# Layer 0's attention ends: the splits of the fetched head outputs stand behind the third scores, one between two stages each

## The chip, the core and the metric

One core of a Trainium2 chip runs the whole program once. The metric is device time in microseconds (us); lower is better. TensorE (PE) multiplies, VectorE (DVE) and ScalarE (ACT) read PSUM and SBUF, GpSimd (POOL) works on SBUF, and SyncE (SP) issues most of the DMAs. Each engine works through its own list of instructions; engines meet through semaphores.

## The reference

Two trunk layers over 512 latent and 256 context tokens of width 1024: layer 0 mixes tokens by differential attention, layer 1 by neighbourhood attention, each followed by a squared-ReLU MLP, with adaptive shift, scale and gate. Only the end of layer 0's attention matters here:

```python
def diff_attend(q, k, v, lam):
    s = jnp.einsum('bqhmd,bkhmd->bhmqk', q, k).astype(jnp.float32) * ATTN_SCALE
    p = jax.nn.softmax(s, axis=-1)
    w = (p[:, :, 0] - lam * p[:, :, 1]).astype(v.dtype)
    return jnp.einsum('bhqk,bkhe->bqhe', w, v)

def finish(o):
    B, T = o.shape[:2]
    o = rms_norm(o, subln_g) * (1.0 - lam_init)
    return o.reshape(B, T, D_MODEL) @ w_o
```

The output of all eight heads is multiplied by `w_o`, gated, and added to the residual stream.

## The kernel before

Tokens stand in six tiles of 128: tiles 0 and 1 are context (they read 256 keys), tiles 2 to 5 are latent (768 keys). fp32 matmuls are done in three passes over operands split into a rounded high part and the remainder. So a "split" is two operations: ACT copies the high part, then POOL or DVE subtracts it to get the low part.

**Stages.** `head0` works on one head in stages, named by a letter and a tile:

- `Q0a`, `Q0b`: two halves of the projection of tile 0.
- `U0`, `U2`, `U4`: queries and keys of two tiles are transposed on PE (L499) and split; the keys by L444, L445, L446, L448 in turn, once for each of the two maps, ACT and DVE alternating.
- `S`: scores (L517) into the PSUM tile `PS`, of which there is one; then twice a reduce to the maximum on DVE (L522) and an exp on ACT (L523), and on DVE L526, L528 and L529, which combines the two maps.
- `T`: the weights are transposed (L541) in two halves into two `PB` tiles and split (ACT L543, DVE L544).
- `V`: weights times values (L552) into a `PB` tile, read by ACT L555 and DVE L556; then a norm: ACT L559, DVE L290, a power on POOL (L296), DVE L561.
- `O`: the output is transposed (L569, `PB`), scaled by ACT L570, and every second tile goes to DRAM (L575) or, for the last head, is split in place (ACT L782, DVE L783).

There are two `PB` buffers, handed out in turn to T, V and O in the order of the code.

**The output projection.** `project` fetches the outputs of heads 0 to 6 back from DRAM: `x0` to `x6` (L738, on SP, into tiles `N`, of which there are four). `X0` to `X6` split them: ACT L743, then L744, which POOL does for X0, X1, X3, X4 and X6 and DVE for X2 and X5. `P0a` to `P5b` multiply tile by tile (L750): an `a` part takes heads 0 to 2, a `b` part heads 3 to 5, both into the same `PA` tile, of which there are two; behind a `b` part DVE multiplies by the gate (L755) and adds the residual (L756). The matmuls of heads 6 and 7 come later. `B0` splits the fourth tile of output weights (ACT L145, POOL L146) and fetches the two gates (L723, also `N`). `m` and `n` are the halves of a chunk of the modulation matmul (L257, L263; `PA`).

**Order.** The stages stand in strings written by hand. `run` walks a string and emits each word's instructions; apostrophes mean an earlier head, so in `END0`, where no new head begins, `'` is head 7 and `''` head 6. On PE, POOL and SP the instructions keep the order of the string (`PINNED`), and so do the splits `X`; the other instructions of ACT and DVE are placed by a scheduler when the program is built. `END0` is the string behind head 7's projection, and in the profiled execution it runs from about 424 to 502 us.

Of the kernel before, what the change touches and what calls it, by code (L numbers as in the profile page):

```python
# [40 lines left out]
T0'' Q4b' S2'' V0'' n0 T1'' V1'' S3'' T2'' U0' Q5a' Q5b' m2 O0'' S4'' T3'' n2 w0 w1 Q0a U2' O1'' V2''  # L41
S5'' T4'' Q0b c0 w2 V3'' S0' Q1a O2'' V4'' U4' Q1b c1 w3 O3'' T5'' m3 O4'' S1' T0' V5'' c2 V0' n3 S2' T1'
Q2a O5'' Q2b S3' V1' c3 O0' U0 Q3a T2' Q3b Q4a S4' T3' Q4b V2' Q5a T4' S5' O1' V3' Q5b S0 T5' m1 U2"""
END0 = """x0 x1 x2 x3 S1' O2'' O3'' V4'' T0' U4' n1' X0 V5'' T1' X1 S2' O4'' X2 x4 V0' S3' x5 P0a O5'' T2' X3 P1a
X4 V1' O0' S4' X5 B0 P0b m0 V2' O1' x6 P1b T3' n0 P2a T4' S5' P2b O2' P3a V3' V4' P3b m1 T5' P4a O3' n1
X6 P4b V5' P5a P5b O4' O5'"""
CYCLE1 = """w0 w1 Q0a T3'' U4' Q1a c0 w2 V2'' V3'' Q0b S0' Q1b Q2a S1' Q2b Q3a T0' S2' Q4a c1 w3 T1' Q3b S3' V0' U0
Q4b c2 U2 Q5a T2' Q5b c3 V1'"""
LAST1 = """Q0a T3'' U4' Q1a c0 x0 x1 V2'' V3'' Q0b S0' Q1b X0 x2 Q2a S1' Q2b X1 Q3a T0' S2' Q4a T1' Q3b X2 S3' V0'
# [868 lines left out]
def run(order, c, steps, load, split, **others):  # L918


    for word in order.split():
        kind, num, h = word[0], word[1:].rstrip("'"), c - word.count("'")
        if kind == "w":
            load(h + 1, int(num))
        elif kind == "c":
            split(h + 1, int(num))
        elif kind in others:
            others[kind](num)
        elif h in steps:
            steps[h](kind, 2 * int(num[0]) + (num[1:] == "b") if kind == "Q" else int(num))  # L930


def hybrid_block(tc, a, out):
    nc = tc.nc
    with ExitStack() as ctx, ExitStack() as st:
# [19 lines left out]
        with b.psum_phase("psA", **PS_ATTN0):  # L955
# [12 lines left out]
            with tc.manual_schedule(engines=PINNED):  # L968
                heads[1] = b.head0(1, w[1], hT)
                for c in range(2, HEADS0):  # L970
                    if c == HEADS0 - 1:
# [9 lines left out]
                       "X": lambda n: proj["split"](int(n), (nc.gpsimd, nc.vector)[int(n) % 3 == 2])}  # L981
                run(END0, HEADS0, heads, load, split, **mod, **own)
            proj["end"]()
# [146 lines left out]
```

## Time and profile before

| | |
|---|---|
| median of 3 runs | 1902.31 us (1901.79 to 1906.84) |
| profiled execution | 1902.15 us, of which the span is 1899.6 us |
| mean granted TensorE clock | 0.981 |
| busy over the span | PE 94%, DVE 60%, ACT 44%, POOL 43% |
| busy in 424 to 502 us, PE | L750 31.6 us, L552 12.4 us, L517 10.9 us |
| PE idle there ahead of L517 | 9.2 us, until ACT L523 (5.1) or L446 (4.1) |
| PE idle there ahead of L750 | 5.7 us, until ACT L743 (5.1) or DVE L744 (0.5) |

PE is the busiest engine over the whole span, so its idle times and the clock granted to it are what to read in a short stretch. A busy share says little there: which wait ended last, and what stood in the queue of the engine that was waited for, is in the rows in order of time.

### The profile page before, as it was taken

Reading aid. Unit: us, or ns where it says so; the run is one execution under the profiler, and the core shown is the slowest. Engines: PE = TensorE matmul, PEld = TensorE weight load, DVE = VectorE, ACT = ScalarE, POOL = GpSimd, SP = SyncE. Lnnn points to the kernel's source line nnn. Section 1 sums busy time; section 2 is a strip of 40 time slices with the busy share of each in tenths; the row PEclk is TensorE's granted clock in tenths of the full one; section 3 lists DMA queues with packets and bytes.
Section 4 is the critical chain, followed back from the end, with each engine's and each line's share of the span. In section 5 each row is a group of like instructions: output and inputs, shape, how many; then the busy total and the mean of one; then the engine's idle time right before and its main releaser. Section 6 shows DMA issues by size and latency. Waiting matters only on the chain.

```text
span 1899.6 us, 27132 instructions
## 1 busy us (share of the span) xinstructions
PE 1786.5 (94%) x10256; PEld 1563.8 (82%) x10256; DVE 1133.4 (60%) x2158; ACT 833.7 (44%) x1854; POOL 812.6 (43%) x688
## 2 busy tenths in 40 slices
PE   6989999996999999999999998999998989999998
PEld 5878888884789888888888977989897778888886
DVE  4588777885574343343334676777777664444446
ACT  4476767774342212221221245777676342323321
POOL 3755566653224333342432432433345444444443
PEclk9999999997999999999999998999999999999999
DMA  8122222224324443443432132122212323223232
GB/s 329 42 84 78 87 87 87 79 71 169 119 73 136 132 160 111 167 162 116 148 134 85 56 100 64 57 71 74 65 67 89 117 92 97 89 91 109 90 101 76
DMA packets 66499, 197.61 MB, mean 104 GB/s; under 512 B 8192, under 2 KB 23488, under 8 KB 60224
## 3 DMA queue, kind: packets, MB, share of 16 engines
q1 hardware_dynamic: 58608, 186.03, 29.4%
q10 hardware_dynamic: 7760, 9.85, 1.5%
q8 instruction: 80, 1.31, 0.3%
q14 instruction: 51, 0.42, 0.1%
HBM read 180.74 MB, written 15.11 MB: 103 GB/s over the span
## 4 chain that ended last, share of the span: by engine, by line
PE 75%; DVE 11%; ACT 6%; issue 4%; POOL 2%; DMA 2%; ACTq 0%; SPq 0%; POOLq 0%; DVEq 0%
PE PD L830 22%; PE PA L408 14%; PE PA L865 11%; PE PB L865 9%; PE PA L750 4%; PE PA L257 2%; PE PS L517 2%; PE PB L552 2%; PE PQ L398 1%; PE PS L656 1%; PE PB L701 1%; PE PB L541 1%; PE PB L686 1%; DVE Y L423 1%; ACT W L145 1%
## 5 line engine op out<-in xcount | busy, mean ns | idle before, releaser
L146 POOL TENSOR_TENSOR W<-R,W 128x1024 fp32r<-128x1024 f32 x142 | 351.3, 2485 | 540.6 <-ACT W L145 537.0
L830 PE MATMUL PD<-Q,W 128*128 128x384 f32 (+2 forms) x1992 | 396.0, 346 | 2.4 <-DVE Q L334 1.1
L830 PEld LDWEIGHTS PD<-Q,W 128*128 128x128 f32 x1992 | 345.7, 188 | 33.7 <-issue 8.6
L145 ACT ACTIVATE W<-R 128x1024 fp32r<-128x1024 f32 (+1 forms) x172 | 172.7, 1021 | 450.7 <-PE PA L865 193.6
L865 PE MATMUL PA<-W,H 128*128 128x512 f32 x1080 | 275.4, 393 | 4.6 <-POOL W L146 3.0
L865 PEld LDWEIGHTS PA<-W,H 128*128 128x128 f32 x1080 | 200.1, 188 | 51.3 <-issue 4.5
L839 DVE TENSOR_TENSOR N<-N 128x768 f32<-128x768 f32 (+1 forms) x64 | 66.9, 1046 | 279.2 <-ACT N L835 170.4
L865 PE MATMUL PB<-W,H 128*128 128x512 f32 x840 | 209.2, 391 | 0.0
L865 PEld LDWEIGHTS PB<-W,H 128*128 128x128 f32 x840 | 157.4, 188 | 33.4
L408 PE MATMUL PA<-W,Q 128*128 128x384 f32 (+1 forms) x1008 | 174.3, 325 | 0.4 <-DVE H L621 0.4
L408 PEld LDWEIGHTS PA<-W,Q 128*128 128x128 f32 x1008 | 158.6, 191 | 0.7 <-DVE H L621 0.7
L296 POOL TENSOR_TENSOR SQ<-SQ,half 128x4 f32<-128x4 f32 (+1 forms) x96 | 94.7, 988 | 128.9 <-DVE SQ L421 127.7
L842 DVE SCALAR_TENSOR_TENSOR H<-N,H 128x768 fp32r<-128x768 f32 (+1 forms) x64 | 97.9, 1532 | 25.7 <-ACT H L841 25.0
L408 PE MATMUL PA<-WB,H 128*128 128x384 f32 x576 | 110.9, 345 | 0.8 <-DVE Q L469 0.8
L750 PE MATMUL PA<-W,H 128*128 128x512 f32 x384 | 97.5, 404 | 7.9 <-ACT H L743 5.1
L408 PEld LDWEIGHTS PA<-WB,H 128*128 128x128 f32 x576 | 101.1, 192 | 1.8 <-DVE Q L469 1.1
L830 PE MATMUL PD<-H,W 128*128 128x512 f32 (+1 forms) x408 | 94.1, 378 | 2.4 <-DVE SA L290 2.0
L876 DVE TENSOR_TENSOR H<-PA,H 128x512 f32<-128x512 f32 x78 | 53.8, 690 | 69.7 <-PE PA L865 69.7
L750 PEld LDWEIGHTS PA<-W,H 128*128 128x128 f32 x384 | 71.9, 192 | 25.9 <-ACT H L743 5.4
L523 ACT ACTIVATE E<-PS,SA 128x768 f32<-128x768 f32 (+1 forms) x96 | 72.9, 760 | 36.5 <-DVE SA L522 33.6
L830 PEld LDWEIGHTS PD<-H,W 128*128 128x128 f32 x408 | 73.8, 188 | 18.0 <-DVE H L334 2.9
L517 PE MATMUL PS<-Q,Q 128*128 128x256 f32 (+1 forms) x320 | 70.2, 352 | 19.1 <-ACT Q L446 9.9
(210 smaller groups left out, 3052.6 us busy)
## 6 DMA issues: line engine op xcount, KB each, us to landing
R<-in_w_dram SPq DMA_DIRECT2D x128, 512.0 KB
M<-in_wmod_dram SPq DMA_DIRECT2D x48, 1024.0 KB
R<-in_wqa_dram SPq DMA_DIRECT2D x32, 384.0 KB
R<-in_wqb_dram SPq DMA_DIRECT2D x32, 384.0 KB
Y<-in_rpb_dram SPq DMA_DIRECT2D x48, 128.0 KB
bias<-Y SPq DMA_DIRECT2D x48, 128.0 KB
X<-bias SPq DMA_DIRECT2D x8, 768.0 KB
R<-in_woa_dram SPq DMA_DIRECT2D x8, 512.0 KB
```

Source lines behind the costliest of these rows:

```text
L145: high = nc.scalar.activation(w[:, 0, :n], raw, AF.Copy)
L146: low = (eng or nc.gpsimd).tensor_sub(w[:, 1, :n], raw, w[:, 0, :n].bitcast(F32))
L296: nc.gpsimd.tensor_tensor(r, ss, self.half[:, :n], op=ALU.pow)
L408: nc.tensor.matmul(acc[:, :n], hT[kt][:, x, P * i:P * i + P], w[kt // 2][:, y, o:o + n], start=(kt == 0 and p == 0), stop=(kt == KT - 1 an ...
L517: nc.tensor.matmul(s[:, c0:c1], q[:, m, P * i:P * i + P], k[:, m, c0:c1], start=p == 0, stop=p == 1)
L523: nc.scalar.activation(e[:, m, :nk], s, AF.Exp, bias=mx[:, 0:1], accum_out=sm[:, m:m + 1])
L750: nc.tensor.matmul(ps, oHL[h][:, x, c:c + P], w[h // 2][:, y, 512 * (h % 2):512 * (h % 2) + 512], start=(first and h == hs[0] and p == 0), ...
L830: nc.tensor.matmul(ps[:, at:at + b1 - b0], w[kt // 4][:, x, o:o + P], hT[kt][:, y, b0:b1], start=(kt == 0 and p == 0), stop=(kt == KT - 1 ...
L839: nc.vector.tensor_mul(r, r, r)
L842: nc.vector.scalar_tensor_tensor(u[:, 1, :], r, 1.0, u[:, 0, :].bitcast(F32), op0=ALU.mult, op1=ALU.subtract)
L865: nc.tensor.matmul(ps, hd[:, x, P * i - c0:P * i - c0 + P], w[f][:, y, 512 * n:512 * n + 512], start=(f == 0 and p == 0), stop=(f == len(h ...
L876: nc.vector.tensor_add(av, ps, av)
```

## The change

Only the string `END0` changes. The same words stand in it, 62 of them before and after, so no instruction is added or removed.

```diff
-END0 = """x0 x1 x2 x3 S1' O2'' O3'' V4'' T0' U4' n1' X0 V5'' T1' X1 S2' O4'' X2 x4 V0' S3' x5 P0a O5'' T2' X3 P1a
-X4 V1' O0' S4' X5 B0 P0b m0 V2' O1' x6 P1b T3' n0 P2a T4' S5' P2b O2' P3a V3' V4' P3b m1 T5' P4a O3' n1
-X6 P4b V5' P5a P5b O4' O5'"""
+END0 = """x0 x1 x2 x3 S1' O2'' O3'' V4'' T0' U4' n1' V5'' T1' S2' X0 O4'' V0' X1 S3' O5'' T2' X2 x4 V1' x5 P0a
+O0' S4' X3 P1a X4 B0 V2' T3' O1' X5 x6 P0b m0 S5' T4' P1b n0 P2a O2' V3' P2b T5' P3a V4' P3b m1 O3' P4a n1
+X6 V5' P4b P5a P5b O4' O5'"""
```

X0 and X1 move from before S2' to behind it; X2 moves behind S3', X3 behind S4' as its own neighbour; V1' moves ahead of P0a; V2', T3' and O1' ahead of P0b; S5' and T4' ahead of P1b; V5' ahead of P4b.

ACT, from the first split to the last exp of S2', before (`H` is a split output, `Q` the keys, `E` the exps, `W` the weight of `B0`):

```order
L743 ACTIVATE H_5607<-N_5522 128x768
L555 ACTIVATE O_5623<-PB_5610,SA_5368 128x128
L543 ACTIVATE X_5633<-PB_5634 128x256
L743 ACTIVATE H_5639<-N_5524 128x768
L444 ACTIVATE Q_5163<-PC_5585 64x256
L559 ACTIVATE O_5627,SO_5626<-O_5623 128x128
L446 ACTIVATE Q_5163<-PC_5585 64x256
L444 ACTIVATE Q_5163<-PC_5585 64x256
L446 ACTIVATE Q_5163<-PC_5585 64x256
L570 ACTIVATE OT_5664<-PB_5665,subg 128x128
L743 ACTIVATE H_5668<-N_5526 128x768
L523 ACTIVATE E_5642,SA_5643<-PS_5644,SA_5653 128x768
```

The same place now:

```order
L555 ACTIVATE O_5620<-PB_5607,SA_5368 128x128
L543 ACTIVATE X_5630<-PB_5631 128x256
L444 ACTIVATE Q_5163<-PC_5585 64x256
L559 ACTIVATE O_5624,SO_5623<-O_5620 128x128
L446 ACTIVATE Q_5163<-PC_5585 64x256
L444 ACTIVATE Q_5163<-PC_5585 64x256
L446 ACTIVATE Q_5163<-PC_5585 64x256
L570 ACTIVATE OT_5661<-PB_5662,subg 128x128
L523 ACTIVATE E_5636,SA_5637<-PS_5638,SA_5647 128x768
L555 ACTIVATE O_5670<-PB_5665,SA_5497 128x128
L523 ACTIVATE E_5636,SA_5637<-PS_5638,SA_5650 128x768
L743 ACTIVATE H_5658<-N_5522 128x768
```

The three L743 of X0, X1 and X2 are gone from among the key copies and the first exp; X0 stands behind the second exp, and the L145 of `B0`, which stood between the two exps, is later too.

PE, behind the eight score matmuls of S3', before: P0a, O5'', T2', P1a, V1'.

```order
L750 MATMUL PA_5712<-W_4935,H_5607 128x512 x3
L750 MATMUL PA_5712<-W_4935,H_5639 128x512 x3
L750 MATMUL PA_5712<-W_4981,H_5668 128x512 x3
L569 MATMUL PB_5722<-ident,O_5627 128x128
L541 MATMUL PB_5727<-ident,E_5642 128x128 x3
L541 MATMUL PB_5733<-ident,E_5642 128x128 x3
L750 MATMUL PA_5742<-W_4935,H_5607 128x512 x3
L750 MATMUL PA_5742<-W_4935,H_5639 128x512 x3
L750 MATMUL PA_5742<-W_4981,H_5668 128x512 x3
L552 MATMUL PB_5755<-Q_4967,X_5633 128x256 x4
```

Now: O5'', T2', V1', P0a.

```order
L569 MATMUL PB_5705<-ident,O_5624 128x128
L541 MATMUL PB_5710<-ident,E_5636 128x128 x3
L541 MATMUL PB_5716<-ident,E_5636 128x128 x3
L552 MATMUL PB_5727<-Q_4967,X_5630 128x256 x4
L750 MATMUL PA_5744<-W_4935,H_5658 128x512 x3
L750 MATMUL PA_5744<-W_4935,H_5680 128x512 x3
L750 MATMUL PA_5744<-W_4981,H_5722 128x512 x3
```

P1a no longer stands between T2' and V1', and P0a follows V1'. With two `PB` buffers in turn, V1' (`PB_5727`) writes where T2''s first half (`PB_5710`) was.

DVE around the softmax of S3', now (L522 reduces, L561 ends the norm of V0', L544 splits T2', L744 is X2); before, L744 and L561 stood ahead of both reduces:

```order
L522 TENSOR_REDUCE SA_5694<-PS_5685 128x1
L561 SCALAR_TENSOR_TENSOR O_5674<-O_5670,SO_5677,one 128x128
L522 TENSOR_REDUCE SA_5697<-PS_5685 128x1
L544 TENSOR_TENSOR X_5709<-PB_5710,X_5709 128x384
L544 TENSOR_TENSOR X_5709<-PB_5716,X_5709 128x384
L744 TENSOR_TENSOR H_5722<-N_5526,H_5722 128x768
```

L561 moved in between the two reduces, and the L544 that V1' needs stands behind both. On POOL the power for that L561 (L296) stands between the L744 of X0 and that of X1.

## The prediction

> **What bounds the kernel now.** Read the page first: the span, and the chain that ended last.
>
> ```profile
> span 1899.6 us, 27132 instructions
> PE 75%; DVE 11%; ACT 6%; issue 4%; POOL 2%; DMA 2%; ACTq 0%; SPq 0%; POOLq 0%; DVEq 0%
> ```
>
> Three quarters of the chain are TensorE (PE), so a change on ACT, DVE or POOL counts only where PE waits for it. END0 runs from about 424 to 502 us. The windows of that stretch come next (columns: stretch, length, busy PE, PEld, DVE, ACT, POOL, granted clock, DMA share, GB/s).
>
> ```profile
> 430.00:440.00 10.00, 5.52 (x28) 3.80 (x27) 7.34 (x18) 5.50 (x16) 4.68 (x4) 0.81 0.53 182
> 440.00:450.00 10.00, 6.70 (x21) 5.34 (x21) 5.96 (x11) 5.35 (x12) 1.32 (x1) 0.51 0.49 178
> 450.00:460.00 10.00, 7.83 (x39) 5.71 (x37) 6.36 (x10) 5.55 (x13) 6.13 (x4) 1.00 0.29 98
> 460.00:470.00 10.00, 5.39 (x26) 2.90 (x27) 5.24 (x8) 2.11 (x4) 0.51 (x1) 0.50 0.28 67
> 470.00:480.00 10.00, 10.00 (x54) 7.94 (x54) 5.62 (x12) 3.08 (x9) 0.55 (x1) 0.98 0.63 236
> ```
>
> PE is full only from 470 on. Before that it idles, and in two stretches its granted clock is half. Third, PE's own rows in order of time (start, length, instruction, idle time before it and its releaser): V5'', the last two pieces of S2', V0', S3', P0a, S4', the last two pieces of P0b, m0, O1', P1b, T3'.
>
> ```profile
> 431.30 1.70 PE L552 MATMUL PB<-Q,X 128*128 128x256 f32 x12 [0.35 <-DVE O L556]
> 436.19 1.46 PE L517 MATMUL PS<-Q,Q 128*128 128x256 f32 x4 [2.51 <-ACT Q L446]
> 439.27 1.26 PE L517 MATMUL PS<-Q,Q 128*128 128x512 f32 x2 [1.62 <-ACT Q L446]
> 440.39 1.20 PE L552 MATMUL PB<-Q,X 128*128 128x256 f32 x4
> 444.90 2.93 PE L517 MATMUL PS<-Q,Q 128*128 128x512 f32 x8 [3.30 <-ACT E L523]
> 447.63 3.27 PE L750 MATMUL PA<-W,H 128*128 128x512 f32 x9
> 454.80 1.64 PE L517 MATMUL PS<-Q,Q 128*128 128x512 f32 x8
> 463.34 1.22 PE L750 MATMUL PA<-W,H 128*128 128x512 f32 x2 [5.09 <-ACT H L743]
> 465.04 0.80 PE L750 MATMUL PA<-W,H 128*128 128x512 f32 x1 [0.48 <-DVE H L744]
> 466.62 1.94 PE L257 MATMUL PA<-M,silu 128*32 128x256 f32 x16 [0.78 <-DVE T L755]
> 470.84 0.27 PE L569 MATMUL PB<-ident,O 128*128 128x128 f32 x1
> 470.86 2.31 PE L750 MATMUL PA<-W,H 128*128 128x512 f32 x9
> 473.01 0.81 PE L541 MATMUL PB<-ident,E 128*128 128x128 f32 x6
> ```
>
> Two things are to be seen. The waits 2.51, 1.62, 3.30, 5.09 and 0.48 us add up to 13.0 us. And the same eight score matmuls take 2.93 us at half clock (S3') and 1.64 at full (S4'), nine projection matmuls 3.27 and 2.31. So the pot is 13 us of waiting and roughly 5 of slow clock, under 1% of the span. About 0.3% (5.7 us) is what a measurement of this kernel can tell from no change; a third of the pot would have to go.
>
> **Step 1: X0 and X1 leave the key split of U4'.** S2' waits for keys that ACT and DVE copy in turn (L444, L445, L446, L448, twice). ACT, DVE and POOL, in this order:
>
> ```profile
> 432.78 0.84 ACT L743 ACTIVATE H<-N 128x768 fp32r<-128x768 f32 x1
> 434.91 0.37 ACT L444 ACTIVATE Q<-PC 64x256 fp32r<-64x256 f32 x1
> 436.62 0.38 ACT L444 ACTIVATE Q<-PC 64x256 fp32r<-64x256 f32 x1 [0.48 <-DVE Q L448]
> 438.84 0.38 ACT L446 ACTIVATE Q<-PC 64x256 fp32r<-64x256 f32 x1 [1.83 <-DVE Q L445]
> 433.25 0.35 DVE L561 SCALAR_TENSOR_TENSOR O<-O,SO,one 128x128 f32<-128x128 f32 x1
> 436.62 1.72 DVE L561 SCALAR_TENSOR_TENSOR O<-O,SO,one 128x128 f32<-128x128 f32 x1
> 438.38 0.43 DVE L445 TENSOR_TENSOR Q<-PC,Q 64x256 fp32r<-64x256 f32 x1
> 435.87 0.55 POOL L296 TENSOR_TENSOR SO<-SO,half 128x1 f32<-128x1 f32 x1 [0.36 <-DVE SO L290]
> 436.38 1.81 POOL L744 TENSOR_TENSOR H<-N,H 128x768 fp32r<-128x768 f32 x1
> ```
>
> V5'' ends at 433.00; two short ACT operations for V5'' and T1' follow (at most 0.37 each, the length of the L444 beside them), so without the two splits the first L444 starts near 433.6 and not 434.91. One round of the four takes 1.7 (434.91 to 436.62), so the second starts at 435.3. In it DVE's L561 took 1.72 instead of 0.35: it started while POOL ran X1's subtraction and ended with it (436.38 + 1.81 = 438.19). With X1 gone L446 ends near 436.5 and PE's last pair near 437.4, against 439.27 + 1.26 = 440.53. **Gain 3.1.**
>
> **Step 2: X2 and the split of the fourth output weight leave S2''s softmax.** PS has one buffer, so S3' waits for reduce, exp, reduce, exp. The scores end at 440.53 and S3' starts at 444.90: 4.37.
>
> ```profile
> 440.56 0.96 DVE L522 TENSOR_REDUCE SA<-PS 128x1 f32<-128x768 f32 x1 [0.89 <-PE PS L517]
> 442.79 0.96 DVE L522 TENSOR_REDUCE SA<-PS 128x1 f32<-128x768 f32 x1 [1.27 <-ACT E L523]
> 443.85 0.91 ACT L523 ACTIVATE E<-PS,SA 128x768 f32<-128x768 f32 x1
> 445.39 1.02 DVE L529 SCALAR_TENSOR_TENSOR E<-E,SA 128x768 f32<-128x768 f32 x1
> 454.11 0.55 DVE L544 TENSOR_TENSOR X<-PB,X 128x384 fp32r<-128x384 f32 x1
> ```
>
> Two reduces (0.96) and two exps (0.91, and about 0.1 for the accumulator's read) are near 4.0. S3' then starts near 441.4: **gain 3.5 in all.** PE still waits 3 us there.
>
> **Step 3: what comes late next, V1'.** Behind S3' the order is now O5'', T2', V1', P0a. V1' takes the PSUM buffer of T2''s first half, so it waits for that half's L544 on DVE, and DVE is in order: L561, S3''s second reduce, L544. X0 stands on ACT from 441.3 to 442.2. POOL's part of it collides with L529 (441.9 to 442.9, as 0.5 to 1.5 behind the exp above) and ends near 444.7; the power for L561 (0.55, the row at 435.87) ends at 445.2; X1, long ready, follows at once and takes 1.81. That is the situation of 436.38, so L561 ends near 447.2, the reduce (0.96) at 448.2, L544 (0.55) at 448.75. T2' is done by 444.4: **a new wait of 4.3.** It lies between the waits of 2.51 and 5.09 that were followed by half clock, so I take V1' at 1.20 (the row of V0' at 440.39) and P0a at 3.27; with O0' (0.4) S4' starts at 453.6 against 454.80. Of 3.5, **1.2 are left.** At full clock it would be near 452.0.
>
> [...]
>
> **Step 4: X3, X4, X5 and P0b.** S4' ends at 453.6 + 1.64 = 455.25; P1a (2.31) and V2' (1.70) follow, to 459.3. T3''s second half needs the buffer of V2', which ACT reads behind S4''s exps and behind X3 and X4.
>
> ```profile
> 452.93 1.60 ACT L743 ACTIVATE H<-N 128x768 fp32r<-128x768 f32 x2
> 458.18 2.34 POOL L146 TENSOR_TENSOR W<-R,W 128x1024 fp32r<-128x1024 f32 x1
> 458.24 2.42 DVE L561 SCALAR_TENSOR_TENSOR O<-O,SO,one 128x128 f32<-128x128 f32 x1 [0.80 <-POOL SO L296]
> 464.03 0.95 DVE L744 TENSOR_TENSOR H<-N,H 128x768 fp32r<-128x768 f32 x1
> 455.92 0.33 SPq L723 DMA_DIRECT2D N<-gates  x1
> 460.00:461.00 1.00, 0.00 (x0) 0.00 (x0) 1.00 (x2) 0.00 (x0) 0.51 (x1) 0.55 0.00 0
> ```
>
> 455.25 + 4.0 + 1.60 + 0.7 (L555, L556) = 461.5: a wait near 2 for T3' (0.7 is an estimate: two operations of half an L544's size). O1' and P0b begin near 462.3. POOL does X3 behind S4''s L529 (460.8 to 462.6), X4 (to 464.4), then at once the weight split of 2.34 (to 466.75). DVE's L783 and X5 both read two SBUF operands. If L783 slips in when X4 ends, X5 is done at 465.8; if the weight split holds it, as it held L561 at 458.24, at 468.2. P0b so ends at 466.2 to 468.8, against 465.04 + 0.80 = 465.84. But V2' (1.70), T3' (0.81) and O1' (0.27), 2.8 in all, are then done, which before came later. **Net -2.4 to +0.2; I take the middle, -1.1,** since no row shows which of two waiting engines gets in at a boundary.
>
> The queue of SP moves with it: x4 and x5 wait for X0 and X1 on POOL (to 444.7 and 447), needed only from 460 on; the second gate, issued at 455.92 before, waits for X3 (462.6). From 460.00 the DMA engines moved nothing (share 0.00 in the last row), so it takes at most 4.1 and lands by 466.7; L755 behind P0b wants it from 466.2. Cost 0 to 0.5, taken as nothing. x6 now precedes the first piece of x; both are used after P0b.
>
> **Step 5: behind P0b.** m0 waits 0.78 for L755 as before. Then S5' and T4' come ahead of P1b, and between P1b and P2a only n0 is left to cover P1b's L755, where T3' (0.81) stood too. L755 also stands behind S5''s two reduces: 0.1 to 0.9 lost. The half clock, which before lasted from 460 to 470, should last about as long: -1 to +1. **I take +0.6.** From P2a on PE was gapless; V5' now comes before P4b, so O5' and L783 at the end have more cover, worth nothing, since the final blocks wait for DVE's L755 chain, which moves along.
>
> **The sum.** -1.1 + 0.6 = -0.5. The profiled execution took 1902.15 (span 1899.6 and 2.55 around it), 0.16 under the median of 1902.31; so 1901.8 for the median.
>
> **Rivals.** *A, the forecast* (chance 0.57): the early gain is eaten by V1', T3' and X5; 1901.8, own range 1899.5 to 1904.
>
> *B, the gain stays* (0.24): L561 gets its turn ahead of X1. Then S4' keeps the whole 3.5 instead of 1.2 (2.3 more), and X5 takes the lower end of step 4 (1.3 more): -4.1, **1898.2**. For it: DVE's L561 and X1 become ready within 0.1 us of each other. Against it: in both rows, 436.62 and 458.24, POOL was first.
>
> *C, slower* (0.17): the weight split holds L783 and X5 past 466.75. It decides when L783 is not in before X4 ends on POOL (464.4). Step 4 gives +0.2, step 5 +0.9, and because PE then waits 3 us just ahead of m0, half clock goes on through S5' (2.93 against 1.64) and P1b (3.27 against 2.31), 2.2 more. +3.3: **1905.6**. Against it: the weight split is short of a fetch that now starts late, and could be late itself.
>
> *D* (0.02): something not seen here.
>
> [...]
>
> **Numbers.** A, B and C lie inside 0.3% of 1902 at their centres. Faster by over 0.3% needs B and a further 1.6: a third of B, 0.08. Slower by over 0.3% needs C and 2.4 more: a third of C, 0.06. The rest, 0.86, is no change. The range takes in B's centre and C's: 1897.5 to 1905.8.
>
> **What would show it.** Right: U4''s last L446 two to three us earlier, S3' starting 3.5 sooner; a long L561 (over 1.5) behind S3''s first reduce, and PE waiting for L544 before V1'; PE waiting for L556 before T3''s second half; P0b's last matmul released by DVE's L744. Wrong: L561 at 0.35 there (B), a wait for the gate's fetch or for x ahead of L755, or m0 and S5' at half clock to beyond 475 (C).

## The result, and the profile after

The changed kernel takes 1905.50 us (median of 22 runs, 1902.88 to 1907.76), the kernel before 1902.98 beside it (22 runs, 1898.59 to 1906.84). The ratio is 1.0015, 95% interval 1.0008 to 1.0021: slower by 1.5 to 4.0 us. The forecast was 0.5 us less than before. The profiled span is 1902.8 us, 3.2 more than before.

The page, the span and the chain that ended last:

```profile
span 1902.8 us, 27136 instructions
PE 73%; DVE 12%; ACT 7%; issue 4%; DMA 2%; POOL 1%; ACTq 0%; SPq 0%; POOLq 0%; DVEq 0%
```

The chain's shares say nothing of the change: two points of PE went to DVE and ACT. The windows (columns as before) show where the idle time and the half clock went:

```profile
430.00:440.00 10.00, 7.19 (x38) 5.05 (x36) 6.83 (x19) 5.29 (x18) 1.37 (x3) 0.83 0.39 150
440.00:450.00 10.00, 4.70 (x17) 3.70 (x18) 7.16 (x11) 7.27 (x16) 4.71 (x3) 0.66 0.26 67
450.00:460.00 10.00, 9.46 (x46) 7.79 (x44) 5.12 (x12) 4.63 (x12) 0.55 (x1) 0.83 0.48 183
460.00:470.00 10.00, 4.21 (x17) 2.13 (x21) 8.23 (x11) 4.05 (x10) 7.94 (x4) 0.87 0.53 165
470.00:480.00 10.00, 9.52 (x49) 6.50 (x42) 5.47 (x10) 3.13 (x7) 0.00 (x0) 0.79 0.58 217
```

PE is busier to 440 and from 450 to 460, less so from 440 to 450 and from 460 to 470. The half clock has left 460 to 470 in part (0.87 for 0.50) and stands in 470 to 480 (0.79 for 0.98), where PE is nearly full (9.52 of 10.00) and every half-speed matmul is paid.

PE's rows: V5'', the last pair of S2', S3', V1', S4', T3''s second half, the last matmul of P0b, S5', P2a:

```profile
431.81 1.70 PE L552 MATMUL PB<-Q,X 128*128 128x256 f32 x12 [0.34 <-DVE O L556]
437.35 1.26 PE L517 MATMUL PS<-Q,Q 128*128 128x512 f32 x2 [0.67 <-ACT Q L446]
442.70 2.93 PE L517 MATMUL PS<-Q,Q 128*128 128x512 f32 x8 [3.02 <-ACT E L523]
449.70 0.78 PE L552 MATMUL PB<-Q,X 128*128 128x256 f32 x4 [2.60 <-DVE X L544]
453.96 1.65 PE L517 MATMUL PS<-Q,Q 128*128 128x512 f32 x8
461.81 0.55 PE L541 MATMUL PB<-ident,E 128*128 128x128 f32 x3 [2.35 <-DVE O L556]
468.04 0.79 PE L750 MATMUL PA<-W,H 128*128 128x512 f32 x1 [2.35 <-DVE H L744]
471.48 2.88 PE L517 MATMUL PS<-Q,Q 128*128 128x512 f32 x8
478.12 2.35 PE L750 MATMUL PA<-W,H 128*128 128x512 f32 x9 [0.48 <-DVE T L755]
```

V5'' starts at 431.81, before at 431.30: 0.51 that arose ahead of the change, taken off below. Of the waits before, those of 2.51 and 1.62 ahead of S2' have shrunk to 1.42 and 0.67, and that of 5.09 is gone; new are 2.60 (V1'), 2.35 (T3') and 2.35 (X5). S5' runs at half clock.

The working of the forecast goes only to P2a; what lies behind it was put at nothing. But there is a loss at the end of END0, behind P5b. The rows of PE: the L569 of O4' right behind P5b, and the 31st of the final L750, where PE waits for the last time in this stretch. Before:

```profile
500.38 0.27 PE L569 MATMUL PB<-ident,O 128*128 128x128 f32 x1
510.19 6.19 PE L750 MATMUL PA<-W,H 128*128 128x512 f32 x26 [1.36 <-DVE T L755]
```

After:

```profile
501.80 0.27 PE L569 MATMUL PB<-ident,O 128*128 128x128 f32 x1
512.99 7.37 PE L750 MATMUL PA<-W,H 128*128 128x512 f32 x31 [1.37 <-DVE T L755]
```

From the one to the other it took 9.81 before and takes 11.19 now. This stretch is called the **tail** below; the **head** is what runs from V5'' to the end of P5b, 500.38 - 431.30 = 69.08 before and 501.80 - 431.81 = 69.99 now.

**The difference by place:** ahead of V5'' 0.51, head 0.91, tail 1.38, behind it 0.40 (1902.8 - 512.99 against 1899.6 - 510.19). Sum 3.20, the whole difference of the spans. Head and tail, 2.29, are put down to `END0` here. The 0.40 is within what executions differ by: over the fourteen kernels profiled here, what stands behind the tail, where the order strings are the same in all, took 1387.4 to 1391.0 us.

In the tail, ACT copies X6, POOL subtracts it, then makes the power of V5''s norm (L296) and splits weights (L146); DVE adds the residual (L756), then ends V5''s norm (L561). Before:

```profile
495.08 0.85 ACT L743 ACTIVATE H<-N 128x768 fp32r<-128x768 f32 x1 [2.07 <-DMA Q<-in_xin_dram]
495.77 0.69 DVE L756 TENSOR_TENSOR Q<-Q,T 128x512 f32<-128x512 f32 x1
497.85 1.06 ACT L145 ACTIVATE W<-R 128x1024 fp32r<-128x1024 f32 x1
498.13 0.54 POOL L296 TENSOR_TENSOR SO<-SO,half 128x1 f32<-128x1 f32 x1
498.71 0.35 DVE L561 SCALAR_TENSOR_TENSOR O<-O,SO,one 128x128 f32<-128x128 f32 x1 [0.81 <-POOL SO L296]
498.99 5.27 POOL L146 TENSOR_TENSOR W<-R,W 128x1024 fp32r<-128x1024 f32 x2 [0.32 <-ACT W L145]
```

After:

```profile
497.23 0.85 ACT L743 ACTIVATE H<-N 128x768 fp32r<-128x768 f32 x1
498.15 1.84 POOL L744 TENSOR_TENSOR H<-N,H 128x768 fp32r<-128x768 f32 x1 [7.75 <-ACT H L743]
498.64 1.90 DVE L756 TENSOR_TENSOR Q<-Q,T 128x512 f32<-128x512 f32 x1
499.27 1.07 ACT L145 ACTIVATE W<-R 128x1024 fp32r<-128x1024 f32 x1 [1.20 <-PE PA L750]
500.92 4.79 POOL L146 TENSOR_TENSOR W<-R,W 128x1024 fp32r<-128x1024 f32 x2
500.99 2.48 DVE L561 SCALAR_TENSOR_TENSOR O<-O,SO,one 128x128 f32<-128x128 f32 x1 [0.44 <-POOL SO L296]
```

Before, L561 starts 0.28 ahead of the weight split and takes 0.35. Now it starts 0.07 behind it and takes 2.48, until the first of the two splits is done. Counted back from the end of P5b, X6's copy begins at 500.38 - 495.08 = 5.30 before and at 501.80 - 497.23 = 4.57 now. These 0.7 us are what decides, because POOL's weight split needs ACT's copy (L145), and that copy stands in the same place in both: 2.53 ahead of the end of P5b (500.38 - 497.85 and 501.80 - 499.27). Before, the power was done first (498.13 + 0.54 = 498.67, the copy at 498.91), POOL waited 0.32 for the copy, and L561 got in. Now the power ends at 500.95 (499.95 + 1.00), after the copy (500.34), and the split follows at once.

### The profile page after: what moved, and what is told of

It reads as the page before. It is cut to its first block, busy times and chain, and to the rows that moved or that the text cites. A ratio compares the mean times of both kernels' runs of the same rounds, so it can differ in the third digit from the quotient of the medians.

```text
span 1902.8 us, 27136 instructions
## 1 busy us (share of the span) xinstructions
PE 1790.5 (94%) x10256; PEld 1565.7 (82%) x10256; DVE 1137.1 (60%) x2158; ACT 834.0 (44%) x1854; POOL 813.8 (43%) x688
## 4 chain that ended last, share of the span: by engine, by line
PE 73%; DVE 12%; ACT 7%; issue 4%; DMA 2%; POOL 1%; ACTq 0%; SPq 0%; POOLq 0%; DVEq 0%
PE PD L830 22%; PE PA L408 14%; PE PA L865 11%; PE PB L865 9%; PE PA L750 3%; PE PS L517 2%; PE PA L257 2%; PE PB L552 1%; PE PQ L398 1%; PE PS L656 1%; PE PB L701 1%; ACT E L523 1%; PE PB L686 1%; PE PB L541 1%; DVE Y L423 1%
## 5 line engine op out<-in xcount | busy, mean ns | idle before, releaser
L146 POOL TENSOR_TENSOR W<-R,W 128x1024 fp32r<-128x1024 f32 x142 | 350.8, 2481 | 541.8 <-ACT W L145 538.2
L145 ACT ACTIVATE W<-R 128x1024 fp32r<-128x1024 f32 (+1 forms) x172 | 172.7, 1021 | 452.1 <-PE PA L865 193.3
L296 POOL TENSOR_TENSOR SQ<-SQ,half 128x4 f32<-128x4 f32 (+1 forms) x96 | 94.8, 988 | 128.6 <-DVE SQ L421 127.5
L750 PE MATMUL PA<-W,H 128*128 128x512 f32 x384 | 98.1, 406 | 6.4 <-DVE T L755 3.2
L522 DVE TENSOR_REDUCE SA<-PS 128x1 f32<-128x768 f32 (+1 forms) x96 | 74.5, 776 | 29.3 <-PE PS L517 17.9
L750 PEld LDWEIGHTS PA<-W,H 128*128 128x128 f32 x384 | 72.1, 194 | 23.9 <-DVE T L755 5.2
```

Of the source, the lines that this page charges most:

```text
L145: high = nc.scalar.activation(w[:, 0, :n], raw, AF.Copy)
L146: low = (eng or nc.gpsimd).tensor_sub(w[:, 1, :n], raw, w[:, 0, :n].bitcast(F32))
L296: nc.gpsimd.tensor_tensor(r, ss, self.half[:, :n], op=ALU.pow)
L522: nc.vector.tensor_reduce(mx, s, op=ALU.max, axis=AX, negate=True)
L750: nc.tensor.matmul(ps, oHL[h][:, x, c:c + P], w[h // 2][:, y, 512 * (h % 2):512 * (h % 2) + 512], start=(first and h == hs[0] and p == 0), ...
```

## The experiments

Twelve kernels. In the table the ratio is to the kernel before on the same chip (10 or 11 runs each, before 15 to 32; for the changed kernel 22 and 22); head and tail are from one profile each, in us. Kernels that differ only behind P2b have heads within about 0.3 us of each other (after, E1, E5, E12: 69.99 to 70.31; E3, E6: 66.24 and 66.33).

| | ratio (95%) | head | tail |
|---|---|---|---|
| before | 1 | 69.08 | 9.81 |
| after | 1.0015 (1.0008 to 1.0021) | 69.99 | 11.19 |
| E1 V5' back | 1.0025 (1.0016 to 1.0035) | 70.31 | 10.58 |
| E2 fourth weight late | 1.0005 (0.9996 to 1.0014) | 69.55 | 11.18 |
| E3 V1' back | 0.9993 (0.9984 to 1.0002) | 66.24 | 11.18 |
| E4 first part alone | 1.0006 (0.9997 to 1.0015) | 69.52 | 9.87 |
| E5 tail back | 1.0004 (0.9995 to 1.0013) | 70.03 | 9.81 |
| E6 V1' and tail back | 0.9975 (0.9966 to 0.9984) | 66.33 | 9.80 |
| E7 X1, X6 on DVE | 1.0003 (0.9994 to 1.0012) | 69.75 | 10.14 |
| E8 as E6, X1, X6 on DVE | 0.9999 (0.9990 to 1.0008) | 67.35 | 11.85 |
| E9 before with the new tail | 1.0019 (1.0010 to 1.0028) | 75.39 | 11.19 |
| E10 as E6, X4 on DVE | 0.9999 (0.9989 to 1.0009) | 66.81 | 9.82 |
| E11 as E6, X1 on DVE | 0.9985 (0.9977 to 0.9994) | 66.40 | 9.82 |
| E12 T5', O3' back | 1.0005 (0.9996 to 1.0014) | 70.25 | 9.80 |

**E1: V5' back behind P4b.**

```diff
-X6 V5' P4b P5a
+X6 P4b V5' P5a
```

> The changed kernel with one word moved back: P4b stands ahead of V5' again, as before the change. Theory 1 (part of the loss is at the end: with V5' first, the split X6 is late on ACT, and POOL's X6 and the two weight splits behind it hold three of DVE's operations, L756, L561 and L756, where before they held two): the last matmul blocks of heads 6 and 7 come about 1.4 us sooner, only two operations of DVE above 1.8 us are left between 497 and 511 us, and the time is 1.4 us under the changed kernel's, a ratio to the kernel before of about 1.0007. Rival (V5''s place costs nothing, as the prediction had it; the loss lies ahead of P2a): the time stays at a ratio of 1.0014, P5b ends where it did, and so do the blocks behind it.

Both failed as put: the tail shrinks to 10.58, not to 9.8, and the ratio rises to 1.0025, above what either said. X6's copy comes no sooner (4.02 ahead of the end of P5b, 504.51 - 500.49), and L561 is held still:

```profile
506.81 2.30 DVE L561 SCALAR_TENSOR_TENSOR O<-O,SO,one 128x128 f32<-128x128 f32 x1
```

**E2: the fourth output weight fetched and split behind P2b** (new word Y0), not with the gates in `B0`.

```diff
-            weights(3)
+            if l:
+                weights(3)
...
-V3' P2b T5'
+V3' P2b Y0 T5'
```

> The changed kernel, but the fourth output weight is fetched and split (L145, L146) behind P2b and not with B0; the gates are still fetched by B0. Theory 1 (POOL's weight split held X5's subtraction on DVE for 2.2 us, and with it P0b, m0, and half clock through S5'): X5's L744 takes about 0.95 us instead of 3.11, PE's wait of 2.35 us ahead of P0b's last matmul goes to under 0.5, S5' runs at 1.64 instead of 2.88; the time is 2.2 to 3.4 us under the changed kernel's, a ratio to the kernel before of 0.9997 to 1.0003. Rival (another wait takes its place: the gate's fetch for L755, or the split where it stands now hits the end): the wait ahead of P0b's last matmul goes, and another of 1.5 us or more appears ahead of m0 or later; ratio 1.0010 or more.

X5's last matmul of P0b and S5':

```profile
468.41 0.50 PE L750 MATMUL PA<-W,H 128*128 128x512 f32 x1 [0.19 <-DVE H L744]
470.74 1.68 PE L517 MATMUL PS<-Q,Q 128*128 128x512 f32 x8
487.85 1.70 PE L552 MATMUL PB<-Q,X 128*128 128x256 f32 x12 [1.58 <-DVE X L544]
```

The wait of 2.35 is 0.19 and S5' is at full clock: the weight split held X5, and the half clock of S5' went with X5's wait. The other profiles agree: where that wait stands (after, E1, E5, E7, E12: 2.34 or 2.35), S5' takes 2.88 to 2.93; where it does not and S5' follows m0 (E2, E3, E6, E8, E10, E11), 1.66 to 1.68. Counted from V5'', P2b starts 3.70 sooner than in the changed kernel (46.33 against 50.03). The third row is part of the price: the split now stands at T5', V4' waits 1.58 for DVE's L544, a wait that the changed kernel does not have, and only 0.44 of the 3.70 is left at the end of P5b. So each theory is right in part, and the ratio of 1.0005 lies between the two.

**E3: V1' back behind P1a.**

```diff
-X2 x4 V1' x5 P0a
+X2 x4 x5 P0a
...
-X3 P1a X4 B0
+X3 P1a V1' X4 B0
```

> The changed kernel with V1' put back behind P1a. Theory 1 (V1' waited 2.6 us for DVE's L544, which stood behind the L561 that X1's subtraction held): P0a starts right behind T2', waits for X2 only at its third head, and S4' starts about 2 us sooner; the time is 1.5 to 2.5 us under the changed kernel's, a ratio to the kernel before of 1.0001 to 1.0007. Rival (X2, which stands behind the same L561, takes the wait over, and half clock stays): S4' starts less than 0.7 us sooner and the time stays at 1.0012 or more.

P0a's wait for X2, then S4':

```profile
452.62 0.50 PE L750 MATMUL PA<-W,H 128*128 128x512 f32 x1 [1.13 <-DVE H L744]
452.99 1.66 PE L517 MATMUL PS<-Q,Q 128*128 128x512 f32 x8
```

V5'' started at 433.46 there, so S4' comes 19.53 behind it, against 22.15 in the changed kernel: 2.6 sooner. The head is 3.75 shorter, 2.84 shorter than before. Theory 1 holds, and step 3 is right: the move of V1' ate the early gain. The ratio is lower than expected (1.0001 to 1.0007), since X5 no longer meets the weight split either (PE has no wait within P0b; in E6, with the same order up to P2b, X5's L744 takes 0.95) and S5' runs at full clock (1.66).

**E4: the splits moved as changed, V1' behind P1a, and from X5 on the order of before.**

```diff
-X4 B0 V2' T3' O1' X5 x6 P0b m0 S5' T4' P1b n0
+X4 X5 B0 P0b m0 V2' O1' x6 P1b T3' n0 P2a T4' S5'
```

> The first half of the change alone: X0 and X1 behind S2', X2 behind S3', X3 behind S4' as in the changed kernel (V1' behind P1a); from X5 and P0b on the words stand as before the change. Theory 1 (the early moves gain, the later ones lose): S3' starts 2.5 to 3 us sooner than before, S4' about 3, P0b begins when X3 to X5 are through and ends 1.5 to 3 us sooner than before; ratio to the kernel before 0.9985 to 0.9995. Rival (what is gained early is lost again at X3 to X5 whatever the later order, because the splits now start later on ACT and POOL): P0b ends within 1 us of before; ratio 0.9997 to 1.0005.

S4' (V5'' at 433.71), then P0b:

```profile
452.94 1.64 PE L517 MATMUL PS<-Q,Q 128*128 128x512 f32 x8
459.41 0.73 PE L750 MATMUL PA<-W,H 128*128 128x512 f32 x2 [2.30 <-ACT H L743]
461.90 1.65 PE L750 MATMUL PA<-W,H 128*128 128x512 f32 x3 [1.76 <-POOL H L744]
464.19 1.65 PE L750 MATMUL PA<-W,H 128*128 128x512 f32 x3 [0.64 <-POOL H L744]
467.38 0.80 PE L750 MATMUL PA<-W,H 128*128 128x512 f32 x1 [1.54 <-DVE H L744]
```

S4' stands 4.27 sooner than before (19.23 against 23.50 behind V5''), yet P0b ends at the same place (34.47 against 34.54): it waits 6.24 for X3, X4 and X5. That is the rival: here the early gain is lost again. E6 below differs from E4 only between X4 and V4': P0b ends 0.91 later there (35.38 behind V5''), but with V2', T3' and O1' (2.78) done, which fill the wait, and its head is 66.33 against 69.52.

**E5: the changed kernel, from P2b on in the order of before.**

```diff
-P2b T5' P3a V4' P3b m1 O3' P4a n1 X6 V5' P4b
+P2b P3a V4' P3b m1 T5' P4a O3' n1 X6 P4b V5'
```

> The changed kernel up to P2b, then the words in the order of before: P3a V4' P3b m1 T5' P4a O3' n1 X6 P4b V5'. Theory 1 (the order of T5', n1, X6 and V5' itself makes the tail longer, since POOL's X6, power and last weight splits stand against DVE's blend and norm): from the end of P5b to the block of the final matmuls that waits for the third time, 9.8 to 9.9 us as before, and not the 11.2 of the changed kernel; time about 1.4 us under the changed kernel, ratio to before about 1.0007. Theory 2 (the tail is late because of what stands before P2b): it stays at 11.2, and the ratio at 1.0015.

Theory 1 holds: tail 9.81 (511.97 - 502.16), head as in the changed kernel.

**E6: E3 and E5 together.**

> V1' back behind P1a, and the tail in the order of before (both of the other single edits together). Theory 1 (the two costs stand in different places and add up): from V5'' to the end of P5b 66.2 us, then 9.8 to 9.9; time about 1.4 us under the kernel with V1' alone moved back, 2 to 3 us under before, ratio 0.9980 to 0.9990. Theory 2 (what is saved ahead of P2b only makes the tail wait longer for DVE): no further gain over V1' alone, ratio 0.9993.

Both gains stand: head 66.33 (498.06 - 431.73), tail 9.80 (507.86 - 498.06), in sum 2.76 under before; the ratio says 3.0 to 6.5 us. This kernel beats both, 1898.86 us against 1902.42.

**E7: the changed kernel, X1's and X6's subtraction on DVE.** E8 does the same to E6, E11 does it to E6 for X1 alone, E10 to E6 for X4.

```diff
-(nc.gpsimd, nc.vector)[int(n) % 3 == 2]
+(nc.gpsimd, nc.vector)[n in "1256"]
```

> The changed kernel with the subtraction of X1 and of X6 done by DVE instead of POOL, everything else in place. Theory 1 (POOL's long subtractions hold DVE's two-input operations at the places named): the norm's last operation behind S3''s first reduce takes 0.35 instead of 1.78; V1' waits about 0.5 to 1 less, since the subtraction of X1 (0.95 where nothing runs beside it) now stands on DVE itself; in the tail the addition of the residual behind X6 takes under 1 instead of 1.90; time 1 to 2 us under the changed kernel. Theory 2 (DVE is late for its own work): the 0.95 twice on DVE puts V1' and the last blocks as late as now or later, time the same within 0.7 us or longer.

DVE's L561 behind S3''s first reduce, and V1' on PE:

```profile
445.99 0.34 DVE L561 SCALAR_TENSOR_TENSOR O<-O,SO,one 128x128 f32<-128x128 f32 x1
448.61 0.74 PE L552 MATMUL PB<-Q,X 128*128 128x256 f32 x4 [1.96 <-DVE X L544]
```

L561 takes 0.34, V1' waits 1.96 instead of 2.60; the head gains 0.24, the tail 1.05. Theory 1.

> V1' behind P1a, the tail in the order of before, and the subtractions of X1 and X6 on DVE. Theory 1: the gains add up, 3 to 4 us under before, ratio 0.9979 to 0.9984. Theory 2 (DVE, not POOL, sets the pace once V1' no longer waits): no better than without the two on DVE, ratio within 0.0005 of that one.

Neither theory: 0.0024 worse than E6. In the tail DVE's L561 met the weight split again (2.45), and ahead of it ACT's list got a split that waits for its fetch in front of S4''s exp:

```profile
455.37 1.06 ACT L145 ACTIVATE W<-R 128x1024 fp32r<-128x1024 f32 x1 [3.19 <-DMA R<-in_woa_dram]
501.91 2.45 DVE L561 SCALAR_TENSOR_TENSOR O<-O,SO,one 128x128 f32<-128x128 f32 x1 [0.44 <-POOL SO L296]
```

**E9: before, with the new tail** (V3' stands ahead of T5' for its sake).

```diff
-P2b O2' P3a V3' V4' P3b m1 T5' P4a O3' n1 X6 P4b V5'
+P2b O2' V3' T5' P3a V4' P3b m1 O3' P4a n1 X6 V5' P4b
```

> The kernel before up to O2', then the words in the order of the change (T5' ahead of P3a, O3' ahead of P4a, X6 and V5' ahead of P4b). Theory 1 (the tail's order costs its 1.4 us whatever stands ahead of it): from the end of P5b to the block of the final matmuls that waits for the third time, 11.2 us and not the 9.8 of before; time 1.4 us over before, ratio about 1.0007. Theory 2 (it costs only behind the changed first half): 9.8, ratio 1.0000.

Tail 11.19, Theory 1 to the hundredth. The total is larger than expected since S5' stands later in before, so that the early T5' waits 3.00 for its softmax:

```profile
486.82 1.52 PE L541 MATMUL PB<-ident,E 128*128 128x128 f32 x6 [3.00 <-DVE E L529]
```

The profiled execution was also the longest of its eleven, 3.9 over their median, so its head of 75.39 is no measure.

**E10: E6 with X4 on DVE.**

> V1' behind P1a and the tail of before, with the subtraction of X4 on DVE instead of POOL. Theory 1 (POOL's X4 holds V2''s norm, and that one releases O1' and P0b): the norm's last operation there takes 0.35 instead of 1.88, O1' waits 1.2 to 1.5 less than 2.80, P0b ends 1 to 1.5 us sooner; but POOL's weight split then also starts 1.8 sooner, and X5 may meet it. Ratio to before 0.9970. Theory 2 (X4's 0.95 on DVE and the weight split on POOL take it back): P0b ends within 0.4 of where it ended with X4 on POOL, ratio as there, 0.9975 to 0.9985.

```profile
461.64 2.34 POOL L146 TENSOR_TENSOR W<-R,W 128x1024 fp32r<-128x1024 f32 x1
461.71 2.42 DVE L561 SCALAR_TENSOR_TENSOR O<-O,SO,one 128x128 f32<-128x128 f32 x1 [0.69 <-POOL SO L296]
```

With X4 gone the weight split follows the power at once and holds the same L561 for 2.42 instead of 1.88. That speaks for theory 2, but P0b ends 0.49 later than in E6, not within 0.4, and the ratio is worse than either theory said; why is open.

**E11: E6 with X1 on DVE.**

> V1' behind P1a and the tail of before, with the subtraction of X1 alone on DVE. Theory 1 (what made the kernel with X1 and X6 on DVE slower than the one without was X6 and the order that ACT got behind it, not X1): S4' starts 0.5 us sooner, ratio within 0.0004 of the one without. Theory 2 (X1 on DVE does it): the second exp of S4' stands behind the fourth weight's split on ACT and that one waits for its fetch, about 2 us lost; ratio near 0.999.

S4' comes 0.57 sooner (19.04 behind V5'' against 19.61), and head and tail are E6's: Theory 1 in the trace. The ratios, 0.0010 apart, overlap in their intervals and so decide nothing.

**E12: the changed kernel with T5' and O3' back, V5' as changed.**

```diff
-P2b T5' P3a V4' P3b m1 O3' P4a n1 X6 V5' P4b
+P2b P3a V4' P3b m1 T5' P4a O3' n1 X6 V5' P4b
```

> The changed kernel with T5' back behind m1 and O3' back behind P4a, but V5' ahead of P4b as changed. Theory 1 (V5' ahead of P4b is what counts: X6's copy on ACT comes behind V5''s reading, its subtraction on POOL then meets DVE's addition of the residual, and V5''s norm meets the weight split): from the end of P5b to the block of the final matmuls that waits for the third time, 10.9 to 11.2 us; the norm's last operation there takes over 2 us. Theory 2 (T5' and O3' earlier is what counts): 9.8 to 10.0, the norm's last operation 0.35. If both matter, between, near 10.6, as with V5' alone moved back.

```profile
497.48 0.85 ACT L743 ACTIVATE H<-N 128x768 fp32r<-128x768 f32 x1 [0.20 <-issue]
498.23 0.29 ACT L559 ACTIVATE O<-O 128x128 f32<-128x128 f32 x1
501.25 0.35 DVE L561 SCALAR_TENSOR_TENSOR O<-O,SO,one 128x128 f32<-128x128 f32 x1 [0.44 <-POOL SO L296]
501.48 5.26 POOL L146 TENSOR_TENSOR W<-R,W 128x1024 fp32r<-128x1024 f32 x2 [0.26 <-ACT W L145]
```

Tail 9.80: Theory 2. P5b ends at 502.86, so X6's copy begins 5.38 ahead of that, not 4.57: ACT's list has it ahead of V5''s L559, in the changed kernel behind. L561 is then 0.23 ahead of the weight split again. V5' ahead of P4b costs nothing by itself. Which of T5' and O3' counts was not tested apart.

## Why the prediction was wrong

All positions of the changed kernel in the text of this section have the 0.51 taken off; the rows are as in the profile.

**Step 1** said S2' ends at 437.4; it ended at 438.1, a gain of 2.4 instead of 3.1. **Step 2** said S3' starts 3.5 sooner; it was 2.7, 0.8 less. Right in kind.

**Step 3 was right in its mechanism.** L561 took 1.78 (forecast 1.7, until X1's subtraction ends), DVE's L544 released V1', and S4' started at 453.45 against the forecast 453.6. The wait was 2.60 and not 4.3: the forecast had T2' done at 444.4, which is where S3' ends by its own numbers (441.4 + 2.93), and left out O5'' and T2' themselves; T2' was done at 446.59. That S4' fits to 0.15 is luck in part: V1' started 0.44 late (449.19), and V1', P0a and O0' then took 4.26 where 4.87 was taken. The rows that show who held whom, POOL and DVE:

```profile
446.37 1.80 POOL L744 TENSOR_TENSOR H<-N,H 128x768 fp32r<-128x768 f32 x1
446.54 1.78 DVE L561 SCALAR_TENSOR_TENSOR O<-O,SO,one 128x128 f32<-128x128 f32 x1
464.63 2.54 POOL L146 TENSOR_TENSOR W<-R,W 128x1024 fp32r<-128x1024 f32 x1
464.88 3.11 DVE L744 TENSOR_TENSOR H<-N,H 128x768 fp32r<-128x768 f32 x1
```

Four operations of DVE took longer in this trace while POOL ran one of these subtractions: 1.78 for 0.35 (L561) and 3.11 for 0.95 (X5's L744) here, 1.90 for 0.69 (L756) and 2.48 for 0.35 (L561) in the tail.

**Step 4: mechanism right, term mis-sized.** T3' waited 2.35 (forecast 2). P0b's last matmul ended at 468.32, inside the 466.2 to 468.8, but near the upper end: X5 met the weight split (the last two rows: 3.11 instead of 0.95). Net is 468.32 - 465.84 - 2.78 = -0.30, where I took "the middle, -1.1". E2 shows the cause. The gate's fetch cost nothing, as taken: m0 waits 0.79, before 0.78.

**Step 5 failed in two sentences.** That the half clock "should last about as long" counted its length, not what ran in it: S5' cost 2.88 instead of 1.65, and P2a waited 0.48. From P0b's end to P5b's the kernel before took 34.54, this one 32.97 with 2.78 less to do: +1.21 where I took +0.6. Worse, V5' ahead of P4b was "worth nothing, since the final blocks wait for DVE's L755 chain, which moves along". The blocks do wait for that chain, but it does not only move along: L561 and L756 stand in it, and POOL held them (2.48 for 0.35 and 1.90 for 0.69). **This is the step that failed most: 1.38 where I took 0.** E5, E9 and E12 show it by three orders; E12 shows that the earlier T5' and O3', which the forecast left out of account, and not V5', made it so: without them the tail is 9.80 with V5' where the change put it.

The account: -0.30 + 1.21 + 1.38 = +2.29, and 0.8, 0.6 and 1.4 are the errors of the three terms. The ratio says 1.5 to 4.0.

**The rivals.** B was refuted by L561's 1.78. C gave 1905.6, close to the time, but in part for other terms: it has X5 held by the weight split and S5' at half clock, which both came, P1b at half clock too, which did not (2.32), and nothing of the tail. So its number was right in part by accident.

What stays open: the single profiles do not follow the medians to better than about 2 us. E1's ratio says 3.0 to 6.7 over before, its head and tail 2.0; E10's says 2.1 less to 1.7 more, its head and tail 2.3 less.

## What to carry to other kernels

Follow a moved stage to the end of the chain that it feeds, and read the rows there of every engine, even where the moved stage itself has cover: here the largest error stood over 20 us behind the last place that was worked out (P2a at 478, L561 at 501). Where an elementwise operation takes three to seven times its usual length, look at what the neighbouring engine has in the same microseconds; an L561 that started 0.23 ahead of the weight split took 0.35, one that started 0.07 behind it 2.48, so such a place is a risk to be put in the range at its upper end, not in the middle. A gain ahead of a chain of splits is kept only if other work fills the wait for them (E4 and E6: heads 69.52 and 66.33).

## What the runs showed of the hardware

In the profiles of before and after the half clock came in stretches near whole multiples of one length, 3.4 us. In windows of 0.5 us the clock reads 0.50 or 1.00 from 430 to 480, except where it changes. So the half-clock time in a stretch is twice its length times one minus the clock: after, 3.4 + 6.8 (430 to 450), 3.4 (450 to 460), 2.6 + 4.2 = 6.8 (460 to 480); before, 3.8 + 9.8 = 13.6 and 10.0 + 0.4 = 10.4. All are near multiples of 3.4. Read in the windows of 0.5 us, the clock of the changed kernel changes at 436.6, 446.9, 450.3, 453.7, 467.3 and 474.2: the later five stand 3, 4, 5, 9 and 11 times 3.41 behind the first. In E2 the half clock, taken from 430 to 480, was about as long (20.2 us against 20.4 in the changed kernel); it stood elsewhere: from 440.0 to 457.0 (17.0, five times 3.4), on S4' (2.12) and P0a (4.04), and not on S5'. What makes the clock fall or come back is not shown: in the changed kernel no wait of PE from 430 to 480 was longer than 3.02, and the clock fell three times. In the 3.4 us ahead of each fall PE was busy for 1.94, 0.82 and 0.96 us; in the 3.4 us to 460.5, after which the clock stayed full, for 2.36.

POOL is held as well as DVE: the subtraction of 1.80 took 2.43 beside DVE's softmax, the power of 0.55 took 1.00 in the tail.

```profile
443.46 2.43 POOL L744 TENSOR_TENSOR H<-N,H 128x768 fp32r<-128x768 f32 x1 [7.62 <-ACT H L743]
499.95 1.00 POOL L296 TENSOR_TENSOR SO<-SO,half 128x1 f32<-128x1 f32 x1
```

And V5'' started between 431.27 and 434.20 in fourteen profiles, although PE's instructions up to there are the same in all of them: 2.9 us, more than the effect in question, from one execution to the next.
